# A hybrid attention and mLSTM layer in fp32: token-major projections made channel-major and transposed, a pair's last product moved, the mLSTM in halves of a head

## The chip, the cores and the metric

The kernel runs on one core of one Trainium2 chip. The metric is the time of one execution on the device in microseconds, taken on the slowest core, which here is the only one.

## The reference

One layer on 1024 tokens of width 1024, all in float32, cut to what matters:

```python
h = rmsnorm(x, norm_pre)
proj = h @ w_in                                   # 1024 x 6664
qa, ka, va, za, qb, kb, vb, ob, zb, ig, fg, ga, gb = split(proj)
# A: 4 heads of differential attention, head width 2 x 64, causal, with ALiBi
oa = (softmax(q1 k1') - lam * softmax(q2 k2')) @ va
ya = rmsnorm_head(oa) * norm_a * (1 - lam_init) * silu(za)
# B: 4 heads of mLSTM, head width 128, causal, with a state carried on
qb, kb = silu(causal_conv4([qb, kb]))
hb = sigmoid(ob) * mlstm(qb, kb, vb, ig, fg)
yb = rmsnorm_head(hb) * norm_b * silu(zb)
m = sigmoid(ga) * (ya @ w_a) + sigmoid(gb) * (yb @ w_b)
x = x + rmsnorm(m @ w_out, norm_post)
```

va, ob and vb are wanted with tokens on the partitions (token-major): the attention multiplies the transposed probabilities with va, the mLSTM multiplies rows of a chunk of 128 tokens with ob. All other parts of the projection are wanted with channels on the partitions (channel-major).

## The kernel before

TensorE does everything in three passes: each operand is split into a high and a low part (`split`: a copy on ScalarE, a subtraction on VectorE), and high x high, high x low and low x high are summed in PSUM. The large input projection saves an eighth of its products by the method of Strassen and Winograd on 2 x 2 blocks: seven products (`PRODS`) give the four blocks of a result of 256 output columns and 1024 tokens. The sums of weight blocks (`Combos`) run on GpSimd (POOL), the sums of the transposed input (ht1 to ht4, H) are made once. The products go into three PSUM banks X, Y and Z (`Banks`); after a product a bank is copied aside (t) or handed to a `sink`, which adds what was kept and stores the block. Product 6 writes bank Y, which product 4's sink reads.

A `Pair` is such a result with channels on the partitions: 7 products of 12 matmuls 128x512. Its weights are loaded (`load`), the first sums are made (`early`), and two products ahead of its own each product's operand is summed and split (`prep`). The pairs have names: qkb0 to qkb3 are q and k of the four mLSTM heads, qka0 to qka3 those of the attention heads, zb and za the gates behind the heads, g10 to g16 and g00 to g06 the merge gates. `tok_wino` is the same method with tokens on the partitions, in 12 matmuls 128x256 a product.

The stages in the order of time, read from the trace (us):

| stage | from to |
|---|---|
| token pass: norm, transposes of x, vb and the gates' inputs (`tok_pass`) | 0 to 72 |
| output gates ob token-major (`tok_wino`, tiles tX, tY, tZ), with the gate chain (`gate_chain`: gcum, uT, mu, gwT) between its products | 78 to 124 |
| values va token-major | 127 to 170 |
| pair qkb0 | 170 to 189 |
| mLSTM, four heads | 189 to 449 |
| attention, four heads, then the last flip | 449 to 774 |
| merge of a (`merge`, tile mrg, weights maw) | 774 to 817 |
| output product and last norm | 817 to 915 |

The order of TensorE's instructions is the order in which the code issues them (`pin`); the other engines' orders come from a scheduler. The code weaves two things: `fill`, the generators of `run_pairs` and of `merge_b`, and a chain (a head of mLSTM or of attention), which yields how many microseconds of fill it wants before its next step, counted at 2.79 for a product of 12. `weave` pulls that much fill at each step, and `until(name)` pulls fill until a pair is done.

A head of the mLSTM (`mlstm_head`) first runs its convolution on VectorE (tiles pad to cv, four steps for q and for k, then the silu with ScalarE's tanh, th), then the flip of the head before, then 8 chunks of 128 tokens. A chunk has a `lead` (score sT, product sm on VectorE, transpose kT) and a `follow` (num from sm and from the state cn, then raw on VectorE, and the state's update upd). At its end come the sums of squares and a power -0.5 on POOL (stb) and a product with all of raw. A flip transposes raw into yT, multiplies with zs, which is read back from z_d in memory, and writes y to y_d. The merges read y_d back (`load_y`, yr).

Of the kernel before, what the change touches and what calls it, by code (L numbers as in the profile page):

```python
# [31 lines left out]
CONV_STEP = 1.4  # L32
# [6 lines left out]
def kernel(  # L39
# [269 lines left out]
    norm_tile(0)  # L309
    load_x(2)  # L310
    norm_tile(XO[1])
    chunk0 = split_chunk(0, raw0)
    rest = turn_tile(0)
    chunk1 = None
    for n, tt in enumerate(XO):
        if n + 3 < NT:
            load_x(n + 3)
        if n + 2 < NT:
            norm_tile(XO[n + 2])
        if n == 0:  # L320
# [82 lines left out]
    def load_tok(c0):  # L403
        raws = {}
        for n in range(2):
            for kh in range(2):
                r = raw_tile([P, 4, 256], f"t{kh}{n}")
                nc.sync.dma_start(
                    r, w_in_v[:, kh * 4 : kh * 4 + 4, c0 + n * 256 : c0 + n * 256 + 256]
                )  # L410
                raws[kh, n] = r
        s2 = wc_tile([P, 4, 256], "ts2", F32)
        return Combos(raws[0, 0], raws[1, 0], raws[0, 1], raws[1, 1], s2)

    SLOTS = ((12, 13), (0, 1), (2, 3), (4, 5), (6, 7), (8, 9), (10, 11))

    def tok_wino(cb, make_sink):
        ops = []
        for i, (what, _, _) in enumerate(PRODS):
            ops.append(tuple(  # L420
                slot(SLOTS[i][e], [P, 4, 256], f"tw{what}{e}", F32R) for e in range(2)
            ))
            cb.make(what, *ops[i])
        for j in range(4):
            js = slice(j * P, (j + 1) * P)
            banks = Banks(256, "t", make_sink(j))
            for i, (_, h, b) in enumerate(PRODS):
                yield from product(
                    i, banks.bank(b),
                    lambda a, b, k: H[h][b][:, k, js],  # L430
                    lambda a, b, k: ops[i][a][:, k, :],
                )
                banks.after(i)

    def sink_so(j):
        def sink(n, T, kept, bank):
            st = part("so")[:, 0:256]
            if kept is not None:
                nc.vector.tensor_add(st, kept, bank)
            nc.scalar.activation(st, bank if kept is None else st, AF.Tanh, scale=0.5)  # L440
            tok_store(so_d, n, T * 4 + j, st)
        return sink

    def sink_va(j):
        def sink(n, T, kept, bank):
            st = part("va")[:, 0:256]
            if kept is not None:
                nc.vector.tensor_add(st, kept, bank)
            else:
                nc.scalar.copy(st, bank)  # L450
            tok_store(va_d, n, T * 4 + j, st)
        return sink


# [45 lines left out]
    done = set()  # L500

    def run_pairs(pairs):
        steps = [(p, i) for p in range(len(pairs)) for i in range(7)]
        pairs[0].load()
        pairs[0].early()
        for q, i in steps[:2]:
            pairs[q].prep(i)
        for n, (p, i) in enumerate(steps):
            if i == 0 and p + 1 < len(pairs):
                pairs[p + 1].load()  # L510
            if i == 5 and p + 1 < len(pairs):
# [103 lines left out]

    y_d = dp.tile([8, P, S], F32, name="y_d")
    z_d = dp.tile([8, P, S], F32, name="z_d")
    g_d = dp.tile([16, P, S], F32, name="g_d")
    m_d = dp.tile([8, P, S], F32, name="m_d")
    qk_d = [dp.tile([4, P, S], F32, name=f"qk_d{h}") for h in range(4)]  # L620

    def hs_(T):
        return slice(T * 512, T * 512 + 512)

    pads = {}

    def pair_qk_b(h):
        def make():
            pads[h] = [slot(i, [P, S + 4], f"pad{i}_{h}") for i in range(2)]
            for p in pads[h]:  # L630
                nc.gpsimd.memset(p[:, 0:3], 0.0)

            def sink(n, T, kept, bank):
                dst = pads[h][n][:, 3 + T * 512 : 3 + T * 512 + 512]
                if kept is not None:
                    nc.vector.tensor_add(dst, kept, bank)
                else:
                    nc.scalar.copy(dst, bank)
            return sink
        return Pair(f"qkb{h}", QB + h * P, KB + h * P, make)  # L640
# [61 lines left out]
    def mlstm_head(h, extra, before, res):  # L702
# [64 lines left out]
        def follow(c):  # L767
# [12 lines left out]
            if c == NT - 1:  # L780
                return
# [388 lines left out]
```

## Time and profile before

| what | value |
|---|---|
| runs | 915.98, 909.67 and 912.91 us, median 912.91 |
| the profiled execution | 916.78 us |
| its span, first to last instruction | 915.1 us |
| instructions | 13746 |
| mean granted TensorE clock | 0.971 |
| TensorE busy | 852.9 us, 93% |
| VectorE, ScalarE, POOL busy | 564.9, 403.2 and 213.3 us |
| bytes moved | 130.10 MB, 142 GB/s |

The profile is of one execution, so a sum of changes is made against 916.78. Engines are called PE (TensorE matmul), PEld (its weight load), DVE (VectorE), ACT (ScalarE), POOL (GpSimd) and SP (the queue that issues the transfers). L79 before, L81 after, is the line of the helper that issues every matmul, so matmuls are told apart by the names of their tiles. A row of the waits names the tile that waited and what released it, then the sum in microseconds, how often, and the longest. A row of the stretches gives the bounds, the length, busy time and count of the five engines, then the granted clock, the share of the transfer engines and GB/s.

### The profile page before, as it was taken

The numbers are of one execution on the slowest core, as the hardware profiler recorded it, in microseconds if no ns is written. First come the engines' busy times: TensorE is split into PE (matmuls) and PEld (weight loads), VectorE is DVE, ScalarE is ACT, GpSimd is POOL, SyncE is SP. The second block draws the span as 40 slices with busy tenths as digits, with TensorE's granted clock in tenths as the row PEclk, the third lists the DMA queues.
The fourth block names the chain that finished last, engine by engine and source line by source line (L and its number), as shares of the span: only waits on it lengthen the run. The fifth ranks groups of instructions, "written<-read, shape, count | busy, mean of one in ns | idle before, by whom it ended". The sixth has DMA issues, their size and how long they took to land.

```text
span 915.1 us, 13746 instructions
## 1 busy us (share of the span) xinstructions
PE 852.9 (93%) x4948; PEld 751.1 (82%) x4948; DVE 564.9 (62%) x1034; ACT 403.2 (44%) x919; POOL 213.3 (23%) x196
## 2 busy tenths in 40 slices
PE   8895989988989979979999989999998998999997
PEld 7895989977868858858788878888887886889997
DVE  6987271295595785776577576766657664882125
ACT  6554251334344434444466556656657341442111
POOL 1435040241252231342412122331220010000002
PEclk9997999998999989999999999999999999999999
DMA  8513142412152441544652462473367489850006
GB/s 267 171 38 115 50 127 64 150 58 78 60 173 70 138 139 51 168 150 158 199 197 70 161 219 82 145 234 97 111 217 249 169 294 281 301 181 1 1 4 250
DMA packets 108228, 130.10 MB, mean 142 GB/s; under 512 B 8728, under 2 KB 72448, under 8 KB 108160
## 3 DMA queue, kind: packets, MB, share of 16 engines
q1 hardware_dynamic: 108160, 129.23, 44.0%
q8 instruction: 39, 0.64, 0.3%
q14 instruction: 29, 0.24, 0.1%
HBM read 89.32 MB, written 39.88 MB: 141 GB/s over the span
## 4 chain that ended last, share of the span: by engine, by line
PE 69%; DVE 12%; issue 6%; DMA 4%; ACT 3%; POOL 2%; SPq 0%; DVEq 0%; POOLq 0%; ACTq 0%
PE out L79 8%; PE mrg L79 8%; PE tY L79 5%; PE pv L79 4%; PE S L79 3%; DVE cv L727 3%; PE tZ L79 2%; PE pT L82 2%; DMA zs<-z_d 1%; PE num L79 1%; PE qka2Y L79 1%; PE qka3Y L79 1%; PE g16Y L79 1%; PE g02Y L79 1%; PE za0Y L79 1%
## 5 line engine op out<-in xcount | busy, mean ns | idle before, releaser
L79 PEld LDWEIGHTS out<-wo,m 128*128 128x128 f32 x768 | 92.3, 192 | 0.1
L79 PE MATMUL out<-wo,m 128*128 128x256 f32 x768 | 92.3, 283 | 0.0
L886 ACT ACTIVATE p<-p,ast 128x128 f32<-128x128 f32 (+7 forms) x64 | 49.7, 777 | 50.1 <-DVE ast L885 30.5
L879 DVE CUSTOM_DVE_ANT_0 p<-S,gm 128x384 f32<-128x384 f32 (+5 forms) x96 | 50.5, 554 | 31.9 <-PE S L79 31.4
L79 PE MATMUL mrg<-y,maw 128*128 128x512 f32 x192 | 45.8, 400 | 4.3 <-ACT y L113 3.5
L1123 DVE TENSOR_TENSOR o<-out,npost 128x256 f32<-128x256 f32 x32 | 13.6, 424 | 56.2 <-ACT oj L1118 56.2
L79 PEld LDWEIGHTS mrg<-y,maw 128*128 128x128 f32 x192 | 37.1, 194 | 12.8 <-ACT y L113 3.9
L79 PE MATMUL mrg<-y,mbw 128*128 128x512 f32 x192 | 47.0, 395 | 0.0
L1118 ACT ACTIVATE oj<-out 128x256 f32<-128x256 f32 x32 | 12.3, 384 | 71.7 <-PE out L79 71.7
L79 PEld LDWEIGHTS pv<-va,pT 128*128 128x128 f32 x288 | 37.2, 193 | 8.0 <-ACT pT L916 5.5
L727 DVE SCALAR_TENSOR_TENSOR cv<-pad,cols,cv 128x1024 f32<-128x1024 f32 x24 | 42.3, 1773 | 0.0
L79 PE MATMUL pv<-va,pT 128*128 128x128 f32 x288 | 38.3, 279 | 3.4 <-ACT pT L916 3.3
L79 PEld LDWEIGHTS mrg<-y,mbw 128*128 128x128 f32 x192 | 35.4, 188 | 7.0
L79 PE MATMUL S<-kll,qs 128*128 128x384 f32 (+5 forms) x96 | 32.9, 345 | 2.1 <-DMA kll<-qk_d 2.1
L79 PE MATMUL S<-khh,qs 128*128 128x384 f32 (+5 forms) x96 | 32.4, 340 | 0.0
L1010 DVE SCALAR_TENSOR_TENSOR tg<-tg,mrg 128x512 f32<-128x512 f32 x32 | 21.8, 685 | 17.0 <-PE mrg L79 13.2
L900 DVE SCALAR_TENSOR_TENSOR p<-p,ast,p 128x128 f32<-128x128 f32 (+7 forms) x32 | 26.9, 841 | 1.0
L344 POOL TENSOR_TENSOR raw_g<-raw_g 128x512 f32<-128x512 f32 x8 | 12.3, 1542 | 60.7 <-DMA raw_g<-in_w_in_dram 40.1
L951 POOL TENSOR_TENSOR sth<-sth,mhalf 128x8 f32<-128x8 f32 x4 | 6.6, 1648 | 85.1 <-DVE sth L948 85.0
L79 PEld LDWEIGHTS sT<-cv,cv 128*128 128x128 f32 x64 | 12.1, 196 | 17.0 <-DVE cv L734 8.0
L79 PE MATMUL sT<-cv,cv 128*128 128x128 f32 x64 | 13.3, 290 | 13.5 <-DVE cv L734 13.5
L916 ACT COPY pT<-pT 128x512 f32<-128x512 f32 (+3 forms) x48 | 21.4, 474 | 6.5 <-PE pT L82 6.3
(1095 smaller groups left out, 2585.0 us busy)
## 6 DMA issues: line engine op xcount, KB each, us to landing
raw_g<-in_w_in_dram SPq DMA_DIRECT2D x16, 512.0 KB, 4.0
g_d<-g SPq DMA_DIRECT2D x32, 256.0 KB, 2.6
tg<-g_d SPq DMA_DIRECT2D x32, 256.0 KB, 3.7
raw_t<-in_w_in_dram SPq DMA_DIRECT2D x8, 512.0 KB, 4.1
raw_qkb<-in_w_in_dram SPq DMA_DIRECT2D x16, 256.0 KB, 3.3
z_d<-zt SPq DMA_DIRECT2D x16, 256.0 KB, 2.0
zs<-z_d SPq DMA_DIRECT2D x16, 256.0 KB, 4.1
y_d<-y SPq DMA_DIRECT2D x16, 256.0 KB, 2.3
```

The source lines that it names most:

```text
L79: pin(nc.tensor.matmul(*args, **kw))
L82: pin(nc.tensor.transpose(out=out, in_=in_, identity=ident))
L344: nc.gpsimd.tensor_sub(v["s3"], v["a11"], v["s3"])
L727: nc.vector.scalar_tensor_tensor(out=cv, in0=pad[:, t : t + S], scalar=cols[:, t * 8 + blk : t * 8 + blk + 1], in1=cv, op0=ALU.mult, op1=A ...
L879: nc.vector.tensor_tensor_reduce(out=pr[:, n0:n1], in0=pss[:, : n1 - n0], in1=gm[:, (7 - i) * P + n0 : (7 - i) * P + n1], scale=-0.125, sc ...
L886: nc.scalar.activation(pr[:, :nk], pr[:, :nk], AF.Exp, bias=nm, scale=-1.0, accum_out=sth[:, c, i : i + 1],)
L900: nc.vector.scalar_tensor_tensor(out=p0[:, :nk], in0=p1[:, :nk], scalar=st[:, 3:4], in1=p0[:, :nk], op0=ALU.mult, op1=ALU.add,)
L916: nc.scalar.copy(pT[:, j0:j1], pt[:, 0 : (j1 - j0) * P].rearrange("p (j t) -> p j t", t=P))
L951: nc.gpsimd.tensor_tensor(rr, ss, mhalf, ALU.pow)
L1010: nc.vector.scalar_tensor_tensor(out=tg, in0=tg, scalar=1.0, in1=ps, op0=ALU.add, op1=ALU.mult)
L1118: nc.scalar.activation(junk[:, 0:256], ps[:, 0:256], AF.Square, scale=D ** -0.5, accum_out=ssq[:, tt, cc : cc + 1],)
L1123: nc.vector.tensor_mul(orr[:, c0 : c0 + 256], ps[:, 0:256], npost[:, c0 : c0 + 256])
```

## The change

- The output gates ob and the values va are no longer made token-major. They become four pairs (ob0, ob1, va0, va1), channel-major, whose blocks TensorE turns by four transposes 128x128 (tile tkT); tanh or a copy takes them out of PSUM and they go to memory. The turns of a block come after the next product (list `later`).
- Product 6 of a pair comes behind product 0 of the next one (`pair_steps`). The first two pairs' weights are loaded and prepared inside the token pass (`open_pairs`).
- The mLSTM is one chain of 33 steps with 7.0 us of fill each. What was done per head is done per half, four chunks (`half_setup`, `half_end`, `flip_half`), and the convolution of the next head is spread over chunks 2 to 5 of a head, into a second pair of cv buffers. Ahead of it stands `until(qkb of the next head)`, and `until` now takes what it pulled off the fill that the next steps get.
- Attention's steps share out the fill that is left, less 12 us. The loads of y of heads 0 to 2 come inside `merge_b`, and the last head's flip splits y in place (`keep`) without going to memory.
- The pairs are in another order: qkb0 ob0, qkb1 zb0 g10, qkb2 ob1 g12, qkb3 zb1 g14, qka0 va0 g16, qka1 za0 g00, qka2 va1 za1, qka3 g02 g04 g06, 24 instead of 20.

```diff
-CONV_STEP = 1.4
+CONV_STEP = 3.0
+MSTEP = 7.0
+RESERVE = 12.0
...
+        steps = pair_steps(pairs)
+        finished = None
         for n, (p, i) in enumerate(steps):
-            if i == 0 and p + 1 < len(pairs):
+            if i == 1 and 0 < p < len(pairs) - 1:
                 pairs[p + 1].load()
-            if i == 5 and p + 1 < len(pairs):
+            if i == 4 and p + 1 < len(pairs):
                 pairs[p + 1].early()
...
+            flush, later[:] = later[:], []
             yield from pairs[p].run(i)
+            for f in flush:
+                f()
...
+    def pair_steps(pairs):
+        steps = []
+        for p in range(len(pairs)):
+            steps.append((p, 0))
+            if p > 0:
+                steps.append((p - 1, 6))
+            steps += [(p, i) for i in range(1, 6)]
+        steps.append((len(pairs) - 1, 6))
+        return steps
...
+    def pair_tok(col, dst, h0, name, tanh):
+        def make():
+            def sink(n, T, kept, bank):
+                st = part("tk")
...
+                def turn():
+                    pt, o = misc("tkT"), part("tko")
+                    for j in range(4):
+                        turn128(pt[:, j * P : (j + 1) * P], st[:, j * P : (j + 1) * P])
...
+                later.append(turn)
...
+    def mlstm(steps):
+        nchunks = 4 * NT
+        half_setup(0, 1)
+        lead(0, 0)
+        yield next(steps)
+        conv_next = None
+        for n in range(nchunks):
+            h, c = divmod(n, NT)
+            w = next(steps)
+            if n + 1 < nchunks:
+                lead(*divmod(n + 1, NT))
+            yield w * 0.5
+            follow(h, c)
+            if c % 4 == 3:
+                half_end(h, c // 4)
+            if c % 4 == 1 and n > 4:
+                hh, hf = divmod(n // 4 - 1, 2)
+                flip_half(mem["raw"][:, :, 0:P], cols[:, 36 + hh : 37 + hh], 4 + hh, hf)
+            if h < 3:
+                if c == 2:
+                    until(f"qkb{h + 1}")
+                    conv_next = conv(h + 1)
+                if 2 <= c <= 5:
+                    for _ in range(2 if c in (3, 5) else 1):
+                        next(conv_next, None)
+                if c == 5:
+                    drain(conv_next)
+            if c == 2 and n > 4:
+                half_setup(h, 1)
+            elif c == 6 and h < 3:
+                half_setup(h + 1, 0)
+            yield w * 0.5
...
     def until(name):
+        was = pulled[0]
         while name not in done:
             pull(0.01)
+        left[0] -= pulled[0] - was
...
+            if n == 20:
+                ys_a.extend(load_y(0, range(3), YA))
...
+    weave(CONV_STEP for _ in conv(0))
+    until("ob0")
+    half_setup(0, 0)
+    pull(2.0)
+    weave(mlstm(MSTEP for _ in range(4 * NT + 1)))
...
+    flip_half(*before[0], 7, 1)
...
+        supply = (total - pulled[0] - RESERVE) / (4 - h)
...
-    flip(*before)
-    ys_a = load_y(0, ("t2h", "t2l", "t1h", "t1l"))
+    y3 = hp.tile([P, 2, S], F32R, tag=f"h{YA[3]}", name="y3")
+    flip(*before, keep=y3)
```

Three places show what the change moves. The first is VectorE at the end of the token pass. Before, behind the last sums of the input (ht2l to ht4l) it makes the first operands of the token-major products (twa, tws), and the gates' inputs (gt) and the gate chain's first steps (gs) stand between them:

```order
L114 TENSOR_TENSOR ht2l<-t_3_750,ht2h 128x4x128
L114 TENSOR_TENSOR ht3l<-b_3_663,ht3h 128x4x128
L114 TENSOR_TENSOR ht4l<-b_3_664,ht4h 128x4x128
L114 TENSOR_TENSOR twa_928<-raw_t_913,twa_927 128x1024
L303 TENSOR_TENSOR gt<-tok,bif 128x8
L304 COPY vb_7_835<-tok 128x256
L546 SCALAR_TENSOR_TENSOR gs_890<-gt 128x32
L114 TENSOR_TENSOR tws_932<-ts_919,tws_931 128x1024
L548 TENSOR_SCALAR gs_892<-gs_891 128x32
```

After the change, VectorE at the same place:

```order
L116 TENSOR_TENSOR ht2l<-t_3_758,ht2h 128x4x128
L116 TENSOR_TENSOR ht3l<-b_3_671,ht3h 128x4x128
L116 TENSOR_TENSOR ht4l<-b_3_672,ht4h 128x4x128
L116 TENSOR_TENSOR qkb0w_931<-qkb0s_771,qkb0w_931 128x512
L305 TENSOR_TENSOR gt<-tok,bif 128x8
L306 COPY vb_7_862<-tok 128x256
L650 SCALAR_TENSOR_TENSOR gs_917<-gt 128x32
L652 TENSOR_SCALAR gs_919<-gs_918 128x32
```

The operands twa and tws are gone. A split of the first pair's weights (qkb0w) stands ahead of gt, and the gate chain's steps follow one another.

The second place is VectorE at a head's convolution. Before, in head 1, the steps (cv_1, from pad_1) stand between operands of the next pair (g10w, qkb2w), sinks (g, pad_2) and the end of head 0 (stb, raw), ahead of the head's first product with a score (sm, two rows further on):

```order
L727 SCALAR_TENSOR_TENSOR cv_1_2561<-pad_1_2234,cols,cv_1_2561 128x1024
L699 TENSOR_TENSOR raw_2159<-raw_2159,stb_2163 128x4x128 x2
L677 TENSOR_TENSOR g<-g_p_2564,g10Y 128x512
L114 TENSOR_TENSOR qkb2w_2590<-raw_qkb_2437,qkb2w_2590 128x512
L734 SCALAR_TENSOR_TENSOR cv_1_2561<-th_1_2599,cv_1_2561 128x1024
L677 TENSOR_TENSOR g<-g_u_2525,g10Z 128x512
L114 TENSOR_TENSOR qkb2w_2616<-raw_qkb_2440,qkb2w_2616 128x512
L727 SCALAR_TENSOR_TENSOR cv_1_2609<-pad_1_2235,cols,cv_1_2609 128x1024
L114 TENSOR_TENSOR qkb2w_2640<-qkb2s_2587,qkb2w_2640 128x512
L742 TENSOR_TENSOR dt_2557<-mask,dt_2557 128x1024
L734 SCALAR_TENSOR_TENSOR cv_1_2609<-th_1_2654,cv_1_2609 128x1024
L114 TENSOR_TENSOR qkb2w_2666<-raw_qkb_2437,qkb2w_2666 128x512
```

After, on VectorE, the convolution of head 2 (cv_1069, cv_1070 from pad_2) within head 1; ring is the product with the score, raw and cn are the chunk's own:

```order
L748 TENSOR_SCALAR cv_1069<-pad_2_1876,cols 128x1024
L116 TENSOR_TENSOR ob1w_2064<-raw_ob_1931,ob1w_2064 128x512
L750 SCALAR_TENSOR_TENSOR cv_1069<-pad_2_1876,cols,cv_1069 128x1024 x2
L116 TENSOR_TENSOR ob1w_2082<-ob1s_2013,ob1w_2082 128x512
L750 SCALAR_TENSOR_TENSOR cv_1069<-pad_2_1876,cols,cv_1069 128x1024
L748 TENSOR_SCALAR cv_1070<-pad_2_1877,cols 128x1024
L116 TENSOR_TENSOR ob1w_2102<-raw_ob_1929,ob1w_2102 128x512
L758 SCALAR_TENSOR_TENSOR cv_1069<-th,cv_1069 128x1024
L548 TENSOR_TENSOR tk<-ob_p_2080,ob1X 128x512
L116 TENSOR_TENSOR ob1w_2121<-raw_ob_1929,ob1w_2121 128x512
L792 SCALAR_TENSOR_TENSOR ring<-sT,dt 128x128
L750 SCALAR_TENSOR_TENSOR cv_1070<-pad_2_1877,cols,cv_1070 128x1024
```

A chunk's ring now stands in the midst of the next head's convolution, rather than behind its own head's.

The third place is TensorE at a chunk. Before, at head 1's second chunk, with fill (qkb2Y, qkb2Z) on both sides of the score and the transpose:

```order
L79 MATMUL qkb2Y<-ht2h,qkb2w_2640 128x512 x2
L79 MATMUL qkb2Y<-ht2l,qkb2w_2640 128x512
L79 MATMUL qkb2Y<-ht2h,qkb2w_2640 128x512
L79 MATMUL sT<-cv_1_2561,cv_1_2609 128x128
L82 MATMUL kT<-ident,cv_1_2609 128x128
L79 MATMUL qkb2Z<-ht1h,qkb2w_2666 128x512
L79 MATMUL qkb2Z<-ht1l,qkb2w_2666 128x512
L79 MATMUL qkb2Z<-ht1h,qkb2w_2666 128x512 x2
L79 MATMUL qkb2Z<-ht1l,qkb2w_2666 128x512
```

After, on TensorE, at the chunk of head 1 behind the fill that is pulled to finish qkb2 (ob1X, ob1Y):

```order
L81 MATMUL ob1Y<-ht2h,ob1w_2082 128x512 x2
L81 MATMUL ob1Y<-ht2l,ob1w_2082 128x512
L81 MATMUL ob1Y<-ht2h,ob1w_2082 128x512
L81 MATMUL sT<-cv_1071,cv_1072 128x128
L84 MATMUL kT<-ident,cv_1072 128x128
L81 MATMUL num<-vbh,ring 128x129
L81 MATMUL num<-cn,qi 128x129
L81 MATMUL upd<-vbh,ring 128x129
L81 MATMUL sT<-cv_1071,cv_1072 128x128
L84 MATMUL kT<-ident,cv_1072 128x128
L81 MATMUL ob1Y<-ht2h,ob1w_2082 128x512
```

The whole of one chunk and the start of the next now stand here with no fill between sT and num. At the other chunks fill stands there as before.

More of the change, by code (lines that the diff above doesn't have):

```diff
@@ L400, in product @@
                 yield 1.4 if bank.shape[1] > 256 else 0.71
[L403 to L452, printed above, removed]
     class Pair:
@@ new lines, in open_pairs, with hs_ @@
+    def open_pairs(pairs):
+        for p in pairs[:2]:
+            p.load()
+        pairs[0].early()
+        for q, i in pair_steps(pairs)[:2]:
+            pairs[q].prep(i)
+    y_d = dp.tile([8, P, S], F32, name="y_d")
+    z_d = dp.tile([8, P, S], F32, name="z_d")
+    g_d = dp.tile([16, P, S], F32, name="g_d")
+    m_d = dp.tile([8, P, S], F32, name="m_d")
+    qk_d = [dp.tile([4, P, S], F32, name=f"qk_d{h}") for h in range(4)]
+    def hs_(T):
+        return slice(T * 512, T * 512 + 512)
@@ new lines, with pair_qk_b @@
+    pads = {}
+    def pair_qk_b(h):
+        def make():
+            pads[h] = [slot(i, [P, S + 4], f"pad{i}_{h}") for i in range(2)]
+            for p in pads[h]:
+                nc.gpsimd.memset(p[:, 0:3], 0.0)
+            def sink(n, T, kept, bank):
+                dst = pads[h][n][:, 3 + T * 512 : 3 + T * 512 + 512]
+                if kept is not None:
+                    nc.vector.tensor_add(dst, kept, bank)
+                else:
+                    nc.scalar.copy(dst, bank)
+            return sink
+        return Pair(f"qkb{h}", QB + h * P, KB + h * P, make)
@@ new lines, in pair_qk_a, with make, sink @@
+    def pair_qk_a(h):
+        def make():
+            def sink(n, T, kept, bank):
+                src = bank
+                if kept is not None:
+                    src = part("qa")
+                    nc.vector.tensor_add(src, kept, bank)
+                hi, lo = part("qah", F32R), part("qal", F32R)
+                split(src, hi, lo)
+                for e, t in enumerate((hi, lo)):
+                    nc.sync.dma_start(qk_d[h][2 * n + e][:, hs_(T)], t.bitcast(F32))
+            return sink
+        return Pair(f"qka{h}", QA + h * P, KA + h * P, make)
@@ new lines, in flip_half @@
+    def flip_half(raw, ncol, slot_, hf, keep=None):
+        until(f"z{'ab'[slot_ // 4]}{slot_ % 4 // 2}")
+        pt = misc("yT")
+        zs, y = part("zs"), part("y")
+        nc.sync.dma_start(zs, z_d[slot_][:, hs_(hf)])
+        for j in range(4):
+            turn128(pt[:, j * P : (j + 1) * P], raw[:, hf * 4 + j])
+        nc.vector.scalar_tensor_tensor(
+            out=y, in0=pt, scalar=ncol, in1=zs, op0=ALU.mult, op1=ALU.mult
+        )
+        if keep is None:
+            nc.sync.dma_start(y_d[slot_][:, hs_(hf)], y)
+        else:
+            split(y, keep[:, 0, hs_(hf)], keep[:, 1, hs_(hf)])
@@ L613, in gate_chain @@
         shared.update(u_c=u_c, em_c=em_c, wk_c=wk_c, dec_c=dec_c, gw_d=gw_d)
[L616 to L640, printed above, removed]
@@ L792, in mlstm_head @@
[L792 to L802 removed]
+                out=cns[:, c], in0=cns[:, c - 1], scalar=dec_c[:, hc : hc + 1],
+                in1=pu_[:, 0 : P + 1], op0=ALU.mult, op1=ALU.add,
+            )
@@ L960, in pull @@
             try:
-                due -= next(fill[0])
+                got = next(fill[0])
+                due -= got
+                pulled[0] += got
             except StopIteration:
```

401 lines of the change are left out of this document (200 added, 201 removed).

## The prediction

> **What bounds the kernel now.** I read the shares of busy time first, then the chain that ended last, then TensorE's waits, and last the granted clock in the stretches behind the longest waits.
>
> ```profile
> PE 852.9 (93%) x4948; PEld 751.1 (82%) x4948; DVE 564.9 (62%) x1034; ACT 403.2 (44%) x919; POOL 213.3 (23%) x196
> ...
> PE 69%; DVE 12%; issue 6%; DMA 4%; ACT 3%; POOL 2%; SPq 0%; DVEq 0%; POOLq 0%; ACTq 0%
> ```
>
> TensorE (PE) is busy for 852.9 of the span's 915.1 us, so some 62 us are all that better order can give, plus what a low clock costs. VectorE (DVE) has 12% of the chain: there TensorE waits for it. Which waits these are, the second view tells (waiting tile, releaser: us in total, times, longest):
>
> ```profile
> PE sT L79 <- DVE cv L734: 13.5, 4, 6.1
> PE tY L79 <- DVE twa L114: 6.1, 1, 6.1
> PE g10Y L79 <- DVE g L677: 3.6, 1, 3.6
> PE mrg L79 <- ACT y L113: 3.5, 1, 3.5
> PE g14Y L79 <- DVE g L677: 3.5, 1, 3.5
> PE xT L82 <- DVE x L218: 3.4, 3, 1.9
> PE pv L79 <- ACT pT L916: 3.3, 4, 2.5
> PE g00X L79 <- DVE qa L648: 3.2, 1, 3.2
> PE tY L79 <- DVE so L439: 2.8, 1, 2.8
> PE qkb3Y L79 <- DVE qkb3w L114: 2.7, 1, 2.7
> PE S L79 <- DMA kll<-qk_d: 2.1, 1, 2.1
> PE tY L79 <- ACT t_p L369: 1.8, 1, 1.8
> PE uT L85 <- DVE u_c L568: 1.4, 1, 1.4
> ```
>
> Four of them start a head of the mLSTM (sT waits for the end of the convolution), three belong to the token-major products (tY), three to a pair's end or start in the mLSTM (g10Y, g14Y, qkb3Y). The last product of a pair is the third writer of bank Y, so it waits for the sink that still reads the bank: g10Y and g14Y.
>
> **The change part by part.** A wait costs more than itself: behind it the clock is low for a while. I price that as (1 - granted clock) times the stretch; the clock is the third number from the end of a row, the stretch's length the first behind its bounds.
>
> *Token-major stages.* The three stretches behind the waits tY and uT:
>
> ```profile
> 77.00:84.00 7.00, 4.55 (x24) 4.35 (x25) 5.94 (x7) 2.34 (x5) 4.66 (x1) 0.74 0.81 242
> 84.00:90.00 6.00, 5.46 (x34) 5.26 (x32) 2.21 (x4) 2.10 (x4) 3.93 (x2) 0.72 0.40 111
> 124.00:140.00 16.00, 13.17 (x98) 12.96 (x98) 10.70 (x11) 5.33 (x10) 5.58 (x3) 0.89 0.61 174
> ```
>
> The waits are 6.1 + 1.8 + 1.4 + 2.8 = 12.1 us, the clock costs 0.26 x 7 = 1.8, 0.28 x 6 = 1.7 and 0.11 x 16 = 1.8, 17.4 in all. The weights of the first pair are now loaded and split before the token pass ends (the order on VectorE has the split of qkb0w ahead of the last gt), and VA no longer starts a stage of its own, so tY's waits go. Next late is the gate chain, whose uT still waits for VectorE (1.4, as now), now with the pairs as cover, and the turns (tkT) behind the first head's convolution: I leave 5.3 us, three waits of 1.2 and one slow stretch of 1.7. **-12.1** (-16, were only 1.4 left, to -7.6, were one more wait like so's 2.8 left with its slow stretch).
>
> *The work itself.* OB and VA were 2 x 4 x 7 = 56 products of 12 matmuls 128x256, and become 4 x 7 = 28 of 12 matmuls 128x512:
>
> ```profile
> 106.78 1.42 PE tX L79 x12
> ```
>
> ```profile
> 173.16 2.72 PE qkb0X L79 x12
> ```
>
> 56 x 1.42 = 79.5 against 28 x 2.72 = 76.2: -3.3. New are 64 transposes 128x128 (4 a sink, 16 a pair). Of such, the trace has eight in a row:
>
> ```profile
> 27.67 1.04 PE L82 MATMUL xT<-ident,x 128*128 128x128 f32 x8
> 28.46 0.37 PE L79 MATMUL tok<-wc,h11h 128*128 128x264 f32 x1
> ```
>
> The next matmul starts 0.79 us after the first of the eight: 0.099 each, 64 x 0.099 = +6.3. **+3.0**; with 1.04 / 8 = 0.13 each it is +5.0. The copies out of PSUM are ScalarE's, which is busy for 44%; nothing waits for them before the head that reads the rows back.
>
> The Trainium skill, "TensorE: Matmul & The Clock Gate", Part 4: PE-mode transpose, speaks against this part: it tells of about 275 ns for a 128x128 transpose inside a kernel, and that the full clock isn't granted to transposes. By that the 64 would take an estimated 17.6 us, and the forecast would be 11 us higher. The row above disagrees: eight in a row went at 0.099 us each.
>
> *The mLSTM, 187 to 449 us.* The stage, then the four slow stretches behind its waits:
>
> ```profile
> 187.00:449.00 262.00, 238.75 (x1151) 199.00 (x1151) 182.39 (x277) 112.24 (x258) 86.32 (x63) 0.96 0.37 116
> 209.00:217.00 8.00, 7.77 (x28) 6.42 (x29) 5.55 (x9) 2.51 (x5) 2.07 (x2) 0.70 0.24 87
> 260.00:270.00 10.00, 6.44 (x21) 4.82 (x21) 8.46 (x9) 3.95 (x6) 7.38 (x5) 0.83 0.40 132
> 337.00:350.00 13.00, 12.05 (x46) 9.96 (x47) 6.57 (x12) 4.06 (x11) 2.57 (x2) 0.75 0.29 100
> 404.00:415.00 11.00, 11.00 (x48) 9.02 (x48) 6.82 (x12) 5.24 (x14) 3.29 (x2) 0.84 0.62 199
> ```
>
> Waits 13.5 + 3.6 + 3.5 + 2.7 = 23.3, clock 2.4 + 1.7 + 3.3 + 1.8 = 9.2: 32.5 us. The convolution moves from the head's own start to chunks 2 to 5 of the head before, and product 6 behind the next pair's product 0, which gives its bank 2.72 us more. What is late next is VectorE:
>
> ```profile
> L727 DVE SCALAR_TENSOR_TENSOR cv<-pad,cols,cv 128x1024 f32<-128x1024 f32 x24 | 42.3, 1773 | 0.0
> L734 DVE SCALAR_TENSOR_TENSOR cv<-th,cv 128x1024 f32<-128x1024 f32 x8 | 10.2, 1272 | 1.1 <-ACT th L733 1.1
> ...
> L725 DVE TENSOR_SCALAR cv<-pad,cols 128x1024 f32<-128x1024 f32 x8 | 5.8, 746 | 0.0
> ```
>
> A head's convolution is (42.3 + 10.2 + 5.8) / 4 = 14.6 us of VectorE. All else is (182.4 - 58.3) / 32 = 3.9 us a chunk, so chunks 2 to 5 ask for 15.5 + 14.6 = 30.1 us. TensorE has four steps there of 7.0 us of fill by the planner's 2.79 us a product, 6.8 by the row's 2.72, and about 1.4 us of the chunk's own matmuls and flips: 33 us. That is 91%, and each instruction that is held up counts. I leave one wait of 2.7 us (the size of qkb3Y's) and one slow stretch of 1.7 for each of the three spread convolutions, 13.2. At two places the fill that the kernel pulls early to finish qkb2 and qkb3 leaves a chunk bare: sT, kT, num, num, upd stand in a row on TensorE, and num waits for VectorE's product with the score. Ahead of it stand 9.5 us of fill against 9 to 11 of convolution and splits on VectorE: 1.7 of wait and 1.7 of clock, 6.8 for both. 20.0 of the 32.5 stay: **-12.5** (-27, were only one place of 5.4 left, to 0). The flips by halves, the loads by halves (32 DMAs on SP's queue instead of 16; the transfers' share in this stage is 0.37) and the double buffers lie beside TensorE; without that cover they would show as more waits of the kind of zs or dt, which the upper end holds.
>
> *Attention and its start.*
>
> ```profile
> 449.00:460.00 11.00, 8.88 (x42) 7.35 (x41) 5.99 (x20) 3.95 (x12) 2.93 (x2) 0.84 0.78 237
> 536.00:545.00 9.00, 5.76 (x22) 4.57 (x21) 4.87 (x11) 3.83 (x10) 0.96 (x1) 0.81 0.56 207
> 768.00:785.00 17.00, 12.72 (x49) 9.84 (x48) 9.38 (x14) 4.92 (x8) 0.00 (x0) 0.90 0.84 290
> ```
>
> S waits 2.1 for kll, g00X 3.2, with 1.8 and 1.7 of clock behind: 8.8 us, gone where the loads and the pair's order are earlier. New is the last half's flip right before attention: its transposes (yT) wait for the half's end, four VectorE instructions, the power on POOL (2.2, row below) and the product with it (1.2 to 2.3 for half a head); I estimate 7 us in all, with some 4.5 us of fill over it; behind yT on TensorE's queue stand all scores of head 0. 3.0 + 1.7 and another 1.5 stay. **-2.6** (-8 to +4).
>
> *The tail.*
>
> ```profile
> 762.99 2.42 DMA y_d<-y
> 765.42 5.93 DMA yr<-y_d
> ```
>
> The last head's rows no longer go out (2.42) and back (5.93), and heads 0 to 2 are loaded in the merge of b, beside attention. mrg's 3.5 and the 1.7 of the third window above go: **-5** (-6 to -1: 24 matmuls instead of 48 are left to cover the flip). The three early loads and their splits lie beside attention, where VectorE has room.
>
> *The token pass* has the same instructions, and the first pairs' weights in it; of xT's longest wait, 1.9, I take **-2** as gone with its clock (-3.5, to +2 where POOL's sums of the weights delay VectorE).
>
> Sum: -12.1 + 3.0 - 12.5 - 2.6 - 5 - 2 = -31.2. The profiled execution took 916.78 us, the median of the runs is 912.91, a factor of 0.9958: 916.8 - 31.2 = 885.6, times 0.9958 = **882 us**.
>
> **The rivals.**
>
> *All cover holds:* every term at its low end but the work (+3): -16 + 3 - 27 - 8 - 6 - 3.5 = -57.5, 856 us. For it speaks that 9% of room is left on VectorE even under the convolution; against it that the stage before had more room (182 of 262) and still stalled seven times. It stands for all below 869.
>
> *VectorE becomes the bound of the mLSTM.* One row has min, median and max in ns of the same convolution step:
>
> ```profile
> L727 DVE SCALAR_TENSOR_TENSOR cv<-pad,cols,cv x24: 1271/1281/3420, 188.8 to 396.3; 128x1024 f32<-128x1024 f32 x24
> ```
>
> The same shape takes 1.28 us or up to 3.42, beside POOL's long sums. If each chunk of 2 to 5 meets one more such delay of 1.6 us (the mean to the longest, 1.77 to 3.42), 12 x 1.6 = 19 us come on top: the mLSTM gives +6.5, the sum is -12.2, 901 us. Then the move of product 6 does not do what it says, as the sink is late anyway. The Trainium skill, "SBUF — State Buffer", section "SBUF: two separate sides", has a rule for this: an instruction of VectorE with two inputs in SBUF and one of GpSimd lock a port pair against each other for a whole instruction. The trace's 1.28 and 3.42 agree with it. By that rule the delay comes with POOL's work on the next pairs, which the change spreads over these same chunks.
>
> *The other side: the end of a half stops VectorE.* The power of half_end runs on POOL, and VectorE's next instruction waits for it:
>
> ```profile
> L814 POOL TENSOR_TENSOR stb<-stb,mhalf 128x8 f32<-128x8 f32 x4 | 8.7, 2184 | 7.3 <-ACT qkb3w L113 3.9 <-DVE stb L811 3.4
> L344 POOL TENSOR_TENSOR raw_g<-raw_g 128x512 f32<-128x512 f32 x8 | 12.3, 1542 | 60.7 <-DMA raw_g<-in_w_in_dram 40.1
> ```
>
> It takes 2.2 us, perhaps behind two sums of 1.5: 5.3 us in which sinks, splits and the next chunk's product stand behind it on VectorE, now 8 times rather than 4. If the fill over it runs dry, each costs 5.3 + 1.7 of clock: 56 us, sum +24.8, 938 us. The change loses from 31.2 / 8 = 3.9 us each. Against it: the halves' ends have a chunk's fill over them, and of the four ends before none is in the list of waits.
>
> **How the numbers follow.** My forecast (869 to 899) 0.60, all cover 0.13, VectorE the bound (899 to 912) 0.19, the halves' ends 0.08. The range of 864 to 906 leaves out most of the first rival, some of the second and all of the third, about 0.2. 1%, 9 us, is about what a measurement of this kernel can tell from no change: faster by more (under 903.8) 0.13 + 0.60 + 0.10 of the 0.19 = 0.83; same, the other 0.09 and 0.02 of the halves' ends at a lower price, 0.11; slower 0.06.
>
> **What would show it.** Right: no waits of tY or twa, no sT wait over 3 us, product 6 of the g pairs not among the waits, 64 tkT transposes near 6 us, yr gone from the end's chain, and a clock of 0.98 in the mean. Wrong: VectorE over 85% busy in the chunks with the convolution and TensorE waiting for ring or cv there; waits of yT or kT at a half's end; tkT above 0.13 us each. The prediction as a whole fails if TensorE's busy time itself grows, since all but 3 us of it is argued from waits.

## The result, and the profile after

The changed kernel takes 874.53 us in the median of four runs (872.15 to 879.27), the kernel before 914.44 (909.67 to 916.7). The ratio is 0.9577, with a 95% interval of 0.9515 to 0.9638: 4.2% faster. The forecast was 882 us, in a range of 864 to 906. The profiled execution took 876.60 us, 40.2 less than that of before, where the sum had said 31.2.

From the page after the change, the busy time of the engines and the chain that ended last:

```profile
PE 842.7 (96%) x4676; PEld 725.2 (83%) x4676; DVE 566.7 (65%) x1057; ACT 402.3 (46%) x922; POOL 211.2 (24%) x206
...
PE 66%; DVE 12%; DMA 9%; issue 6%; ACT 3%; POOL 2%; SPq 1%; DVEq 0%; POOLq 0%; ACTq 0%
```

TensorE is busy 842.7 of 874.8 us. Its idle time fell from 62.2 to 32.1 us, and its busy time by 10.2 although its work grew, because the mean granted clock rose from 0.971 to 0.995. VectorE's busy time is the same within 2 us. The waits after the change:

```profile
PE tkT L84 <- DVE tk L548: 5.2, 4, 2.6
PE xT L84 <- DVE x L220: 3.7, 3, 1.6
PE mrg L81 <- DVE tg L1084: 2.7, 1, 2.7
PE pv L81 <- ACT pT L987: 2.2, 4, 1.4
PE qka3X L81 <- DVE z L522: 1.8, 1, 1.8
...
PE g00Y L81 <- DVE g L537: 0.9, 1, 0.9
PE kT L84 <- DVE ring L792: 0.8, 1, 0.8
PE zb1Y L81 <- DVE z L522: 0.8, 1, 0.8
PE num L81 <- DVE cn L829: 0.7, 1, 0.7
...
PE yT L84 <- DVE raw L852: 0.2, 1, 0.2
```

No tY is left, no sT, no g10Y, g14Y or qkb3Y. New are tkT, the turns, which wait for VectorE's sum of the block, and a wait of mrg in the tail. Five stretches after: the new pairs with head 0's convolution, the convolutions of heads 1, 2 and 3 (the last two with a bare chunk), and the merge of a.

```profile
72.00:118.00 46.00, 41.60 (x188) 32.85 (x187) 35.57 (x56) 21.23 (x41) 17.85 (x12) 1.00 0.38 100
...
135.00:175.00 40.00, 39.61 (x196) 32.83 (x195) 33.81 (x53) 19.26 (x43) 11.69 (x10) 1.00 0.42 125
200.00:240.00 40.00, 38.51 (x199) 32.04 (x198) 31.45 (x49) 17.61 (x42) 11.83 (x10) 1.00 0.35 106
270.00:310.00 40.00, 38.40 (x188) 31.63 (x187) 36.48 (x52) 18.32 (x41) 14.63 (x9) 1.00 0.36 107
...
735.00:778.00 43.00, 40.17 (x173) 32.12 (x172) 34.18 (x54) 15.36 (x24) 0.00 (x0) 0.96 0.74 250
```

From 270 to 310 us VectorE is busy for 36.5 of 40 us, 91%, which is the share that the prediction had worked out for all three convolutions; in the two stretches before it is 85 and 79%. TensorE still lost only 1.6 us where VectorE was busiest, at full clock.

One thing was overlooked ahead of the result: the change also drops the line that pins TensorE to the order of the code, so its order now comes from the scheduler. The order shown ahead of the prediction is the scheduler's, so the working had the right rows; the experiment "order pinned" below tells what the line is worth.

### The profile page after: what moved, and what is told of

It reads as the page before. It is cut to its first block, busy times and chain, and to the rows that moved or that the text cites. A ratio compares the mean times of both kernels' runs of the same rounds, so it can differ in the third digit from the quotient of the medians.

```text
span 874.8 us, 13183 instructions
## 1 busy us (share of the span) xinstructions
PE 842.7 (96%) x4676; PEld 725.2 (83%) x4676; DVE 566.7 (65%) x1057; ACT 402.3 (46%) x922; POOL 211.2 (24%) x206
## 4 chain that ended last, share of the span: by engine, by line
PE 66%; DVE 12%; DMA 9%; issue 6%; ACT 3%; POOL 2%; SPq 1%; DVEq 0%; POOLq 0%; ACTq 0%
PE out L81 9%; PE mrg L81 7%; PE pv L81 4%; PE S L81 3%; DMA zs<-z_d 2%; PE pT L84 2%; DVE cv L750 2%; PE tok L81 1%; PE qka1Y L81 1%; PE za0Y L81 1%; PE g02Y L81 1%; PE qkb1Y L81 1%; PE va1Y L81 1%; PE qkb2Y L81 1%; PE qka0Y L81 1%
## 5 line engine op out<-in xcount | busy, mean ns | idle before, releaser
L81 PEld LDWEIGHTS pv<-va,pT 128*128 128x128 f32 x288 | 36.5, 191 | 7.4 <-ACT pT L987 5.3
L750 DVE SCALAR_TENSOR_TENSOR cv<-pad,cols,cv 128x1024 f32<-128x1024 f32 x24 | 37.9, 1580 | 0.1
L971 DVE SCALAR_TENSOR_TENSOR p<-p,ast,p 128x128 f32<-128x128 f32 (+7 forms) x32 | 29.2, 913 | 1.0
L324 POOL TENSOR_TENSOR raw_g<-raw_g 128x512 f32<-128x512 f32 x8 | 10.4, 1299 | 80.2 <-DMA raw_g<-in_w_in_dram 69.4
L1194 POOL TENSOR_SCALAR ssq<-ssq 128x1 f32<-128x1 f32 x8 | 2.8, 352 | 82.0 <-ACT oj L1187 82.0
L576 DVE SCALAR_TENSOR_TENSOR y<-yT,cols,zs 128x512 f32<-128x512 f32 x16 | 12.0, 747 | 16.3 <-DMA zs<-z_d 16.3
L84 PE MATMUL pT<-ident,p 128*128 128x128 f32 x144 | 21.1, 274 | 1.4 <-DVE p L971 1.4
```

Of the source, the lines that this page charges most:

```text
L81: pin(nc.tensor.matmul(*args, **kw))
L84: pin(nc.tensor.transpose(out=out, in_=in_, identity=ident))
L324: nc.gpsimd.tensor_sub(v["s3"], v["a11"], v["s3"])
L576: nc.vector.scalar_tensor_tensor(out=y, in0=pt, scalar=ncol, in1=zs, op0=ALU.mult, op1=ALU.mult)
L750: nc.vector.scalar_tensor_tensor(out=cv, in0=pad[:, t : t + S], scalar=cols[:, t * 8 + blk : t * 8 + blk + 1], in1=cv, op0=ALU.mult, op1=A ...
L971: nc.vector.scalar_tensor_tensor(out=p0[:, :nk], in0=p1[:, :nk], scalar=st[:, 3:4], in1=p0[:, :nk], op0=ALU.mult, op1=ALU.add,)
```

## The experiments

### The parts of the mLSTM

**Product 6 back in its own pair.**

```diff
-            steps.append((p, 0))
-            if p > 0:
-                steps.append((p - 1, 6))
-            steps += [(p, i) for i in range(1, 6)]
-        steps.append((len(pairs) - 1, 6))
+            steps += [(p, i) for i in range(7)]
```

> The changed kernel, with product 6 of a pair back at the end of its own pair, all else as changed. Theory (the move pays): product 6 waits for the sink of product 4 on bank Y with only product 5's 2.7 us as cover, and VectorE is 91% busy where the convolution runs (36.5 of 40 us from 270 to 310), so three to six waits of 1 to 3.5 us come back with one or two slow stretches of 1.7: 6 to 15 us, 880 to 890 us. Rival (the spread convolution alone removed these waits, since before they stood behind a convolution in one piece): at most one such wait, 873 to 878 us.

Measured: 872.08 us (871.67 to 872.21), ratio 0.9559 (0.951 to 0.9608). In the waits those for a bank are back (ob1Z, on bank Z, is not a product 6):

```profile
PE zb0Y L81 <- DVE z L518: 3.4, 1, 3.4
PE zb1Y L81 <- DVE z L518: 3.0, 1, 3.0
PE ob1Z L81 <- ACT ob_p L349: 2.7, 1, 2.7
PE g12Y L81 <- DVE g L533: 1.3, 1, 1.3
```

The theory was right on the waits, 7.7 us of product 6, and wrong on the time. The changed kernel's own idle time is 32.1 us, that of this kernel 870.3 - 839.8 = 30.5: here the wait of mrg (2.7, with a slow stretch behind it) is missing, as are pv, pT and qka3X (5.4 together in the changed kernel), and tkT waits 3.4 instead of 5.2. Moving product 6 gives no time that can be measured here. Whether these differences follow from the edit or from the execution isn't settled.

**The next head's convolution in one piece at chunk 5, and late, after chunk 6.**

```diff
-                if c == 2:
+                if c == 5:                      # the second kernel: c == 6
                     until(f"qkb{h + 1}")
-                    conv_next = conv(h + 1)
-                if 2 <= c <= 5:
-                    for _ in range(2 if c in (3, 5) else 1):
-                        next(conv_next, None)
-                if c == 5:
-                    drain(conv_next)
+                    drain(conv(h + 1))
```

> The changed kernel, with the next head's convolution issued in one piece at chunk 5 instead of spread over chunks 2 to 5 (it waits for the same pair there). Theory (the spread pays): 14.6 us of VectorE stand ahead of the next chunk's product with the score and of the fill's sinks, against some 7 to 9 us of fill on TensorE: 5 us of wait and 1.7 of slow clock at three places, +20 us, 890 to 898 us. Rival (the double buffers and the early place alone do it, the queue orders itself by what is ready): under 878 us, no wait over 1.5 us more.

> The changed kernel, with the next head's convolution issued after chunk 6, so that one chunk with 7 to 10 us of fill stands between it and the next head's first score. Theory (what pays is that the convolution is done well ahead): 14.6 us of VectorE and more among it against 7 to 10 of fill, sT waits 4 to 7 us at three heads and 1.7 of slow clock behind each: 890 to 900 us. Rival (TensorE's fill is enough however late it comes): under 879 us.

Measured: 871.5 us (868.95 to 875.57) in one piece, 873.35 (869.46 to 875.99) late. Both rivals hold: neither edit costs anything that can be measured. Why, the first step of the convolutions of heads 1 to 3 shows (ns min/median/max, then the first and last start in us), after the change, in one piece, and late:

```profile
L748 DVE TENSOR_SCALAR cv<-pad,cols x6: 740/747/755, 137.9 to 281.7; 128x1024 f32<-128x1024 f32 x6
```

```profile
L748 DVE TENSOR_SCALAR cv<-pad,cols x6: 741/746/756, 139.0 to 283.1; 128x1024 f32<-128x1024 f32 x6
```

```profile
L748 DVE TENSOR_SCALAR cv<-pad,cols x6: 735/743/753, 138.9 to 283.4; 128x1024 f32<-128x1024 f32 x6
```

They start within 2 us of each other. VectorE's order is the scheduler's, and it takes the convolution when its input and its buffer are there, wherever the code issues it. The spread over chunks 2 to 5 in the code is thus not what keeps the scores from waiting.

**The late convolution with one pair of cv buffers.**

```diff
-        mem["cv"] = [[slot(i, [P, S], f"cv{i}") for i in ab] for ab in ((2, 3), (9, 11))]
+        mem["cv"] = [[slot(i, [P, S], f"cv{i}") for i in ab] for ab in ((2, 3),)] * 2
```

> The kernel with the late convolution (issued after chunk 6), and one pair of cv buffers for all heads instead of two: the next head's convolution can begin on VectorE only when chunk 7's score and transpose have read the buffers, and the next head's first score comes one step of 7 us of fill later. Theory (what the rebuilt mLSTM gains from is the second pair of buffers, which lets the scheduler take the convolution ahead wherever the code issues it): three waits of sT of 6 to 10 us with 1.7 to 3 of slow clock behind each, +22 to +36 us on the late convolution's 873, 895 to 909 us. Rival (the halves, or the fill of 7 us a chunk, do it): under 882 us.

Measured: 885.58 us (883.33 to 889.78), ratio 0.971 (0.9676 to 0.9745), 12.2 more than the late convolution with two.

```profile
L748 DVE TENSOR_SCALAR cv<-pad,cols x6: 742/744/746, 171.1 to 314.6; 128x1024 f32<-128x1024 f32 x6
```

```profile
PE g14Z L81 <- DVE g14w L116: 3.1, 1, 3.1
PE g10Z L81 <- DVE g10w L116: 3.1, 1, 3.1
```

Now the convolution starts 32 us later. The second buffers are what lets it move ahead. The price lies between the theory's 22 to 36 and the rival's: sT waits only 0.8 us, and the time goes at the splits of the next pair's weights (g10w, g14w), which stand behind the convolution on VectorE. In the two profiles idle time is 8.0 us more and busy time 2.0.

**More fill under the convolution of the kernel before**, CONV_STEP 2.0 instead of 1.4.

> The kernel before, with 2.0 instead of 1.4 us of fill under each of a convolution's nine steps (18 instead of 12.6 us a head; a head's 49 us of fill stay, so a chunk gets 3.4 instead of 4.0). Theory (the mLSTM's gain is a matter of how much fill stands ahead of a head's first score): the four waits of sT, 13.5 us, fall to under 2 and half of the slow clock behind them goes, 895 to 901 us. Rival (it takes the place a head ahead and the second buffers, more fill only moves the wait to sinks and chunks): 907 to 914 us.

Measured: 909.71 us (907.65 to 916.04), ratio 0.9977 (0.9949 to 1.0005): no difference. The waits show a move:

```profile
PE qkb3Y L79 <- ACT zb1w L113: 5.5, 1, 5.5
...
PE g10Y L79 <- DVE g L677: 3.5, 1, 3.5
PE g14Y L79 <- DVE g L677: 3.5, 1, 3.5
...
PE zb0Y L79 <- DVE z L662: 2.8, 1, 2.8
```

The 13.5 us of sT have gone from the list of waits, qkb3Y has grown from 2.7 to 5.5, and zb0Y is new. In the mLSTM the waits add up to 17.2 us instead of 23.3, so over half of the 13.5 turned up at other tiles, and the slow clock stays: by stretches of 5 us, (1 - clock) times length is 10.3 us there, against 10.2. The reading that fits is that VectorE's whole queue is late at the start of a head, not the score alone, and that covering one consumer hands much of the wait to the next.

**As much fill in the mLSTM as before**, MSTEP 5.94 instead of 7.0, on the kernel with later turns (below, 871.79 us).

> The kernel with the later turns (871.8 us), with 5.94 instead of 7.0 us of fill a chunk: 33 x 5.94 = 196 us over the four heads, as much as the kernel before had (4 x 49), and 35 us more left for attention. Theory (the mLSTM's other gain is more fill over the same work of VectorE, some 182 us): waits of ring, num and of the pairs' sinks come back in the mLSTM, 6 to 15 us more, 878 to 887 us. Rival (the arrangement does it: work by halves and the second buffers take the bulges out of VectorE's queue, and 196 us cover it): 869 to 875 us.

Measured: 883.44 us (881.01 to 884.85), ratio 0.9678 (0.965 to 0.9705), 11.6 slower, inside the theory's range, but not by its way. In the mLSTM no wait is over 1.8 us (yT) and the clock stays at 1.00; its waits add up to 7.3 us, 4.1 more than in the kernel with later turns. The other long waits stand in attention and the tail:

```profile
PE mrg L81 <- DVE tg L1089: 6.8, 2, 4.5
...
PE yT L84 <- POOL oa L727: 3.5, 3, 2.6
PE pT L84 <- DVE p L976: 3.0, 2, 1.9
PE yT L84 <- DVE raw L857: 2.9, 3, 1.8
```

So the mLSTM keeps most of its gain with before's fill: the arrangement makes that, as the rival had it, though its time was off. The 35 us of fill did not go to attention, as the expectation had it. The code pulls fill until va0 is done before attention starts, so 39 us of it run between the last chunk (its num at 343.6 us) and the first score (382.7), where the kernel with later turns has 5.5. Why attention and the tail wait longer behind it is not shown, and was in neither theory.

**More work for VectorE**: the first step of the convolutions of heads 1 to 3 nine times.

```diff
-            nc.vector.tensor_scalar(cv, pad[:, 0:S], cols[:, blk : blk + 1], None, ALU.mult)
+            for _ in range(1 if h == 0 else 9):
+                nc.vector.tensor_scalar(cv, pad[:, 0:S], cols[:, blk : blk + 1], None, ALU.mult)
```

> The changed kernel, with the first step of the convolutions of heads 1 to 3 done nine times instead of once (16 instructions of 0.75 us more a head on VectorE, 12 us, the result the same): VectorE is asked for some 42 us in chunks 2 to 5, where TensorE has 33. Theory (VectorE is near its limit there, as the prediction had it): 9 us a head more, +27 us, 898 to 906 us. Rival (work of VectorE may run on into chunks 6, 7 and the next head, where it has room, and only the few instructions that TensorE waits for count): +3 to +10 us, 877 to 885 us.

Measured: 892.27 us (892.07 to 892.91), 17.7 more.

```profile
PE 848.2 (95%) x4676; PEld 729.1 (82%) x4676; DVE 601.4 (67%) x1105; ACT 402.1 (45%) x922; POOL 215.1 (24%) x206
```

VectorE has 34.7 us more, of which half came through to the time, between the two theories. So VectorE is near its limit in the mLSTM, and half of the added work is hidden. That it runs on into the chunks that have room, as the rival has it, fits this, but no run shows where it went.

### The other parts

**Output gates and values token-major again**, in the changed kernel (`tok_wino`, `load_tok` and their sinks as before, ahead of 20 pairs; no turns).

```diff
+    cb = load_tok(OB)
+    cb.early()
+    fill.append(tok_wino(cb, sink_so))
+    weave(gate_chain())
+    pull(1000.0)
+    cb = load_tok(VA)
+    cb.early()
+    drain(tok_wino(cb, sink_va))
...
+    open_pairs(pairs)
     fill.append(run_pairs(pairs))
...
-    weave(gate_chain())
```

> The changed kernel, but with the output gates and values token-major again, in two stages of their own ahead of the pairs as before (20 pairs, no turns, the first pair's weights loaded after these stages). Theory (the stages' waits are one part of the gain by themselves): the waits of tY and uT, 12 us, and some 4 of slow clock come back, the turns' 6.6 and tkT's 5.2 go, the products cost 3.3 more: +7 to +11 us, 881 to 886 us. Rival (the four more pairs were the fill that covers the mLSTM and attention): new waits there and later, over 890 us. Other rival (a wash): under 878 us.

Measured: 888.67 us (888.03 to 890.08), ratio 0.9737 (0.9682 to 0.9792), 14.1 more than the changed kernel.

```profile
PE tY L81 <- DVE twa L116: 4.2, 1, 4.2
PE sT L81 <- DVE cv L808: 4.1, 1, 4.1
PE tZ L81 <- ACT tws L115: 3.6, 1, 3.6
PE g06Y L81 <- DVE g L589: 3.6, 1, 3.6
PE tY L81 <- DVE so L419: 2.8, 1, 2.8
PE qka0Y L81 <- DVE qka0w L116: 2.2, 1, 2.2
PE yT L84 <- DVE raw L902: 2.2, 1, 2.2
```

The stages' waits come back, as the theory had it, and with them one wait of sT at head 0, 4.1 us, whose convolution has lost its cover. Three more stand outside the stages: qka0Y, yT ahead of attention, and g06Y late in attention, 8.0 us together, of which the changed kernel has 0.2. So the result is more than the theory's 7 to 11, and part of it is the first rival's, which says that the four pairs were cover for what follows.

**Each turn twice.**

```diff
-                    for j in range(4):
+                    for j in [0, 1, 2, 3] * 2:
```

> The changed kernel, with each of the 64 transposes of ob and va done twice in a row (the result is the same). Theory: a transpose costs 0.10 us in a row of four, so +6.5 us, 881 us, no more waits. Rival by the Trainium skill's figure of 275 ns for one: +17.6 us, 892 us. Second rival: TensorE has idle room there anyway (waits of tkT 5.2 us), so +1 to 3 us.

Measured: 881.41 us (879.13 to 883.8), 6.9 more, 0.108 a transpose. In the changed kernel four of them take 0.41 us, from 101.51 to the next matmul's start:

```profile
101.51 0.66 PE L84 MATMUL tkT<-ident,tk 128*128 128x128 f32 x4 [1.10 <-DVE tk L548]
101.92 0.48 PE L81 MATMUL ob0Z<-ht1h,ob0w 128*128 128x512 f32 x1
```

The theory holds. The estimate of 17.6 us by the Trainium skill's 275 ns ("TensorE: Matmul & The Clock Gate", Part 4: PE-mode transpose) does not. One transpose takes 272 ns here too, in the median, but four in a row take 0.41 us to the next matmul's start: they overlap, and the duration of one is not what one more of them costs.

**The last head's y through memory.**

```diff
-    y3 = hp.tile([P, 2, S], F32R, tag=f"h{YA[3]}", name="y3")
-    flip(*before, keep=y3)
-    ys_a.append(y3)
+    flip(*before)
+    ys_a.extend(load_y(0, range(3, 4), YA))
```

> The changed kernel, with the last head's y written to memory and read back again before the merge of a. Theory: the write (2.4 us) and the read (5.9 us) stand in the way of the merge's last operand with some 5 us of fill over them: a wait of mrg of 3 to 5 us and 1.7 of slow clock, 878 to 882 us. Rival: the merge waits a little later anyway (2.7 us for tg, behind the split of wo on ScalarE), and the delay is taken up there: 874 to 876 us.

Measured: 882.93 us (882.14 to 886.68), 8.4 more, with one wait of this size:

```profile
PE mrg L81 <- ACT maw L115: 10.9, 1, 10.9
```

It is more than the theory's 3 to 5. Only 24 matmuls are left behind the flip, and they end at 726.5 us, where the write only starts. The chain has the write and, last, the load of the merge's own weights (raw_ma):

```profile
726.60 2.73 DMA y_d<-y
...
729.72 6.88 DMA raw_ma<-in_w_a_dram
```

The read of y (raw_yr) is issued at 729.35 and landed by 735.1; the weights' load behind it lands 1.5 us later, at 736.6. In the changed kernel the last of these loads is issued at 713.6. So the round trip has no cover, and it holds up the weights as well.

**Turns two products later.** The list of turns goes through one product more.

```diff
-            flush, later[:] = later[:], []
+            held = list(later)
+            later.clear()
             yield from pairs[p].run(i)
-            for f in flush:
+            for f in ripe:
                 f()
+            ripe[:] = held
...
```

> The changed kernel, with each block's turn two products behind its sink's product instead of one (2.7 us more for VectorE's sum into tk; ob and va count as done when their last turn is out). Theory (the waits of tkT, 5.2 us in all and 1.7 of slow clock in some runs, are VectorE's sum coming late): they go, 867 to 870 us. Rival (the longer hold of the tk tiles, which share five buffers with all other staging tiles, delays sinks instead): 873 to 877 us.

Measured: 871.79 us (869.61 to 872.28), ratio 0.955 (0.9525 to 0.9575). The waits of tkT fall from 5.2 us to 0.2. Against the changed kernel this is 2.7 us, less than the spread of its runs, and against the next one, on the same chip, 5.4. Its median is level with those of the convolution in one piece (871.5) and of product 6 back (872.08), and none of the three is shown by intervals to be faster than the changed kernel.

**TensorE's order pinned.**

```diff
+    ordered[0] = True
     PAIR, MB = 7 * 12 * 0.2325, 16 * 12 * 0.2325
```

> The changed kernel, with TensorE's order pinned to the order of the code as in the kernel before (the change drops that line; by the order on TensorE six places move, each by one to a few instructions). Theory: no difference, 872 to 878 us. Rival (the free order steps round waits at the bare chunks): 2 to 4 us slower, with waits of num at the two bare chunks.

Measured: 877.23 us (873.61 to 881.33), ratio 0.9618 (0.9588 to 0.9647). This is in the theory's range, and also 2.7 us over the changed kernel, in the rival's; the spread of both can't tell them apart. The waits of num add up to 1.7 us instead of 0.7, less than the rival needs. The free order thus explains 3 us of the gain at most by the medians, and none of it is shown.

## Why the prediction was right, point by point

The terms as they came out, priced as in the prediction (waits plus low clock by stretch), in us:

| term | forecast | in the profile after |
|---|---|---|
| token-major stages | -12.1 | 17.4 became 4.4, tkT 3.7 and two short ones: -13.0 |
| work, turns | +3.0 | 64 x 0.103 - 3.3: +3.3 |
| mLSTM | -12.5 | 32.5 became 4.4, no slow clock: -28.1 |
| attention's start | -2.6 | 8.8 became 2.8 (g00Y, qka3X): -6.0 |
| tail | -5 | 5.2 became 4.4 by a new wait: -0.8 |
| token pass | -2 | -1.4 |
| sum | -31.2 | -46.0 |

The kernel gained 40.2, so the terms add up to 5.8 too much. The reason lies in the price of the clock. By stretches of 5 us, (1 - clock) times length comes to 26.3 us before and 4.2 after, 22.0 less; but TensorE's busy time fell by 10.2 with 3.3 us more work, so 13.5 us is what the clock gave. A stretch that holds part of the wait itself counts that idle time a second time: taken on TensorE's busy time alone, the same stretches come to 18.9 before and 2.9 after, 16.0 less. In the table the clock stands at about 19.6 (5.3 + 9.2 + 3.5 + 1.7 before against 1.7 after, and 3.4 against 1.8 in the token pass), 6.1 more than the 13.5. Without these the terms come to -39.9.

That the sum came within 9 us of the gain is in part luck. The mLSTM gave 15.6 us more than its term, while the tail gave 4.2 less and the price of the clock was 6.1 too high in the table.

**The token-major stages and the work** came out by their own steps, within 1 us, but in an execution without the slow stretch that six other kernels show at the turns (last section); with its 1.7 us the first term would be -11.3. A turn costs 0.108 us by experiment and 0.103 by the trace. The stages are not priced by the experiment alone: taking both terms back cost 14.1 us, where they come to 13.0 - 3.3 = 9.7, and it brought waits outside the stages as well.

**The mLSTM** is the term that was mis-sized: of 32.5 us I let 20.0 stay, 4.4 did. The step that failed is "one wait of 2.7 us (the size of qkb3Y's) and one slow stretch of 1.7 for each of the three spread convolutions", and the same again for the two bare chunks. VectorE's share was near, 91% at one convolution and 85 and 79% at the others. But no convolution has a wait of 2.7 us or a slow stretch, and of the 6.8 us for the bare chunks only kT's 0.8, in the second, is there. A queue that was 91% busy made next to no wait: the few instructions that TensorE needs can stand at the right places in it. That the scheduler puts them there once the second buffers let the long ones go ahead is the reading that fits the run with one buffer. The added load shows the size: half of it is hidden. By that, I estimate that the rival's 19 us of delay would have cost near 10. What the second buffers are worth is shown for the late convolution: 12 us of time, against 28 in the term. That the halves make the rest is only argued, since no experiment took them back. Less fill cost the mLSTM 4.1 us of waits, more fill in the kernel before and the place of the convolution's code gained nothing that can be measured, and the four pairs seem to cover a part, by sT's 4.1 us without them.

**Attention's start.** The new wait of yT, forecast at 3.0 + 1.7, is 0.2: the cover was enough. The 2.8 us left are of other pairs (g00Y, qka3X).

**The tail** gained little in this execution, because another wait took its place. The rows of ScalarE, VectorE and TensorE there:

```profile
747.04 1.05 ACT L115 CAST wo<-raw_o 128x1024 fp32r<-128x1024 f32 x1 [3.04 <-DMA raw_o<-in_w_out_dram]
...
748.12 1.23 DVE L116 TENSOR_TENSOR wo<-raw_o,wo 128x1024 fp32r<-128x1024 f32 x1 [2.11 <-ACT wo L115]
749.26 0.69 DVE L116 TENSOR_TENSOR m<-tg,m 128x512 fp32r<-128x512 f32 x1
749.86 0.68 DVE L1084 SCALAR_TENSOR_TENSOR tg<-tg,mrg 128x512 f32<-128x512 f32 x1
...
750.60 26.29 PE L81 MATMUL mrg<-y,maw 128*128 128x512 f32 x108 [2.69 <-DVE tg L1084]
```

The split of the output weights (wo) waits on ScalarE and VectorE for its load (raw_o), m and tg stand behind it, and mrg waits for tg's bank. The kernels with product 6 back and with the convolution in one piece don't have this wait; there ScalarE waited 2.2 and 2.0 us for the load, not 3.0. Eight of the other nine have it, with 0.8 us or more. That it hangs on the load's landing is argued from this, not shown. Keeping y in place is still worth 8.4 us, as the round trip has no cover in this tail.

**The rivals.** "All cover holds" came true in the mLSTM (-28.1, where it had -27) and not in the tail. "VectorE becomes the bound" did not happen, though each further microsecond of VectorE there cost about half of one. The delays that this rival adds didn't come either: the same step of the convolution took 3.42 us at the longest and 1.77 in the mean before, 2.32 and 1.58 after. The halves' ends did hold up VectorE, for 10.9 us in 8 waits, but TensorE for only 0.2 us in all (yT):

```profile
L750 DVE SCALAR_TENSOR_TENSOR cv<-pad,cols,cv x24: 1267/1278/2321, 91.0 to 294.7; 128x1024 f32<-128x1024 f32 x24
...
DVE raw L852 <- POOL stb L851: 10.9, 8, 2.2
```

That the move of product 6 does not do what it says had been put under the second rival, for the reason of a late VectorE. It does remove the waits, and still saves no time that can be told.

## What to carry to other kernels

A share of busy time near the limit says that delays are possible, not that they happen: ask which of the queue's instructions the other engine needs, and what keeps the rest from going ahead of them. Where a scheduler sets an engine's order, try a second buffer before a new place in the code: here the one moved the convolution by 32 us and the other by 2. A wait that is covered in one place can turn up at the next consumer of the same late queue, as over half of it did here, so look at the queue before paying for cover. And count a low clock on busy time alone.

## What the runs showed of the hardware

In the profiled executions, a wait of the same length at the same place brought a slow stretch in six kernels and none in a seventh. At 110 us, ahead of a turn, the changed kernel waited 2.6 us, as the kernel with the convolution in one piece did. The 5 us from 110, of the first and of the second:

```profile
110.00:115.00 5.00, 2.36 (x13) 1.74 (x12) 5.00 (x6) 1.30 (x3) 5.00 (x4) 1.00 0.01 3
```

```profile
110.00:115.00 5.00, 2.46 (x8) 2.16 (x9) 5.00 (x5) 1.20 (x2) 4.72 (x4) 0.76 0.08 10
```

The clock stayed at 1.00 in the one, and in the 5 us that follow, and was 0.76 in the other. Five more kernels wait 2.6 us at this turn (the late convolution, with one buffer and with two, the added load, the round trip and the pinned order), and their clock goes down to between 0.66 and 0.77 in one of these two windows. Length doesn't decide it between 1.9 and 3.5 us either. With before's fill, a wait of 1.9 us at pT left a clock of 0.66 from 390 to 395 us, and in the kernel before, g14Y's wait of 3.5 us, up to 393.1, left 1.00. A single slow stretch is thus forecast to no better than its own 1.7 us.
